# A one-core encoder layer: modulation columns of the first chunk moved ahead, later chunks of h made whole from PSUM, and high weights used first

## The chip, the cores and the metric

The kernel runs on one core of a Trainium2 chip, as one launch. The metric is the device time of that launch in microseconds (us). Three runs of the kernel before took 1886.06 to 1887.91 us, with a median of 1886.77 us. The engines are named as in the profile: PE does matrix multiplications and transposes, PEld is its loading of the stationary operand, DVE, ACT and POOL do elementwise work, and SP issues most of the transfers.

## The reference, cut to what matters

The layer mixes a convolution branch and a stick-breaking attention branch. What the change touches is its beginning, up to the projections of q, k and v:

```
mod = silu(c) @ w_ada + b_ada          # 3 x 1024 values, one row
shift, scale, gate = split(mod, 3)
h = rms_norm(x, norm_g) * (1 + scale) + shift      # x is 2048 x 1024, f32
u = h @ w_in                           # 1024 x 5632; 1536 of the columns are q, k, v
q, k = head_rms_norm(q), head_rms_norm(k)
```

All tensors are float32. The kernel keeps that precision by splitting each operand into a high part in PE's rounded format (`fp32r`) and a low part, the remainder, and by adding three products: high with high, high with low, low with high.

## The kernel before, in words

The 2048 positions are worked in four chunks of 512, the last first (ORDER is 3, 2, 1, 0). For each chunk, and for each of the eight blocks kc of 128 channels, h is kept on chip as two tiles of 128 x 512, `hhi` and `hlo`. The weights of q, k and v come in six groups of 256 columns (q0, q1, k0, k1, v0, v1), each in two pieces of four blocks, and each piece as a high and a low tile. `nat_tile` (L211) computes, for half a chunk, two results of 128 positions x 256 columns out of 24 matmuls each.

**The modulation.** Each of the 16 values needed per channel block (`mod` columns 8 + kc for the scale and kc for the shift) is a dot product of a row of `w_ada` with silu(c). `mod_col` does one column on DVE: a multiply of a 128 x 1024 tile `wa` with `ca` whose sum is accumulated. The `wa` tiles come by `wa_load` into a ring of four (NWA).

**The first chunk (the loop over kc in the middle of `trunk_kernel`).** In each turn the two columns of block kc are done on DVE, then ACT makes `b_s` and `a_s` from them, then `hf` (the modulated block, from PSUM), then `hhi`; DVE then makes `hlo`, and PE multiplies the block with q0 and q1 (24 matmuls of 128 x 256). DVE and ACT are written with `dve` and `act`, which keep the program's order on those engines, so that the next block's columns stand behind this block's `hlo`. The weights of q0 and q1 are cast (ACT) and their low parts taken (DVE) between.

**The later chunks.** `h_half` makes half a chunk (two tiles of 128 positions): the squares of x on ACT, a reciprocal square root of ten small steps on DVE (`rsqrt`), a scaling of each x tile, PE's transposes into PSUM (`x_block`, a ring of three banks, `pt`), and then `modulate` for each block of 128 x 256: `hf` on ACT from PSUM (L386), `hhi` as a cast of `hf` on DVE (L393), `hlo` on POOL (L394; on DVE for some blocks). Two halves make a chunk. Chunk 2 is made while k0 and k1 are computed for chunk 3, chunk 1 during v0 and v1, chunk 0 during the first q matmuls of chunks 2 and 1. POOL also takes the low parts of the k and v weights (L103).

What sets the order is a scheduler that takes the program's order as priority; in the built program the order on each engine is fixed. A transfer takes one of eight completion counters in turn, and waits for the transfer that had the counter before it.

After that the kernel has three long stages that the change leaves alone: the projections and the convolution (to about 800 us), attention with the remaining projections beside it, and the output projections.

## Time and profile before

| | |
|---|---|
| median of three runs | 1886.77 us |
| profiled execution | 1884.81 us |
| its span on the core | 1883.1 us |
| PE busy in the span | 1800.1 us (96%) |
| DVE, ACT, POOL busy | 1240.0, 818.6, 682.1 us |

The span is the time from the first to the last instruction in the trace; the profiled execution is 1.7 us longer, which lies around the span. A busy PE is a modelled number: matmuls overlap, and a matmul's row lasts longer than the distance to the next one. Where the rows of matmuls stand one behind the other, the distance of their starts is what one of them costs. The granted clock of PE is shown as a share of 2.4 GHz, so that 1.00 is the upper and about 0.5 the lower of its two levels.

### The profile page before, as it was taken

How to read it: one execution, taken by the hardware profiler on the slowest of the kernel's cores; microseconds unless marked ns; L12 is line 12 of the kernel's file. 1: busy time of each engine (PE TensorE's matmuls, PEld its weight loads, DVE VectorE, ACT ScalarE, POOL GpSimd, SP SyncE). 2: the span in 40 equal slices, each digit the busy share in tenths (PEclk: the TensorE clock that was granted, in tenths of full speed). 3: DMA queues.
4: the chain of work that ended last, by engine and by line, in shares of the span. 5: the costliest groups of instructions: out<-in, count | busy, mean ns of one | idle time of the engine just before them, and what ended most of it. 6: DMA issues, size and time to landing. Idle time of an engine off the chain costs nothing.

```text
span 1883.1 us, 27362 instructions
## 1 busy us (share of the span) xinstructions
PE 1800.1 (96%) x9612; PEld 1519.3 (81%) x9612; DVE 1240.0 (66%) x1757; ACT 818.6 (43%) x1904; POOL 682.1 (36%) x919
## 2 busy tenths in 40 slices
PE   5889999999999998999999999999999899999999
PEld 4788889899898887878877778787788777888887
DVE  6785577997879554467777777777777895334341
ACT  4466113223131122257776776777777753010100
POOL 0253111102112143466666666656666641010100
PEclk9999999999999999999999999999999999999999
DMA  7463511406032443342222323131322346353532
GB/s 270 139 188 106 166 40 37 132 34 173 31 104 93 157 156 118 124 148 76 90 86 78 90 76 96 62 99 65 98 76 88 120 149 218 107 162 95 162 95 79
DMA packets 117599, 211.10 MB, mean 112 GB/s; under 512 B 15442, under 2 KB 27730, under 8 KB 117460
## 3 DMA queue, kind: packets, MB, share of 16 engines
q1 hardware_dynamic: 116308, 207.24, 34.8%
q10 hardware_dynamic: 1152, 2.10, 0.3%
q8 instruction: 76, 1.25, 0.3%
q14 instruction: 63, 0.52, 0.1%
HBM read 137.98 MB, written 71.30 MB: 111 GB/s over the span
## 4 chain that ended last, share of the span: by engine, by line
PE 72%; DVE 9%; issue 6%; POOL 5%; DMA 4%; ACT 4%; SPq 1%; DVEq 0%; ACTq 0%; POOLq 0%
PE pd L115 39%; PE po L115 9%; PE p L115 8%; PE av L115 5%; PE pT L120 5%; PE z L115 5%; POOL w L933 3%; DVE sc L926 2%; POOL wlo L103 1%; ACT z L922 1%; PE pt L120 1%; DVE wa L131 1%; DVE tlo L960 1%; DMA gt<-ga 1%; DMA wl<-in_w_qkv_dram 1%
## 5 line engine op out<-in xcount | busy, mean ns | idle before, releaser
L933 POOL TENSOR_TENSOR w<-w,sc 128x512 f32<-128x512 f32 (+1 forms) x320 | 361.7, 1131 | 252.0 <-DVE sc L926 179.1
L115 PE MATMUL pd<-hhi,whi 128*128 128x512 f32 x1024 | 412.4, 403 | 1.0 <-ACT vsg L839 1.0
L115 PE MATMUL pd<-hhi,wlo 128*128 128x512 f32 x1024 | 402.0, 393 | 0.0
L115 PE MATMUL pd<-hlo,whi 128*128 128x512 f32 x1024 | 401.8, 392 | 0.0
L926 DVE TENSOR_TENSOR_SCAN sc<-z,sc,w 128x512 f32<-128x512 f32 x192 | 245.0, 1280 | 91.3 <-ACT z L922 83.7
L103 POOL TENSOR_TENSOR wlo<-wl,whi 128x512 fp32r<-128x512 f32 x88 | 129.1, 1477 | 404.8 <-ACT whi L102 404.5
L921 ACT ACTIVATE w<-z 128x512 f32<-128x512 f32 (+1 forms) x320 | 172.2, 538 | 126.9 <-PE z L115 101.3
L115 PEld LDWEIGHTS pd<-hhi,wlo 128*128 128x128 f32 x1024 | 193.0, 188 | 42.2 <-POOL wlo L103 0.2
L115 PEld LDWEIGHTS pd<-hhi,whi 128*128 128x128 f32 x1024 | 195.0, 190 | 35.2 <-ACT vsg L839 1.4
L115 PEld LDWEIGHTS pd<-hlo,whi 128*128 128x128 f32 x1024 | 193.7, 189 | 34.1
L960 DVE TENSOR_TENSOR tlo<-pT,thi 128x512 fp32r<-128x512 f32 (+1 forms) x320 | 184.0, 598 | 35.1 <-ACT thi L959 32.4
L115 PE MATMUL z<-kt,q 128*128 128x512 f32 (+2 forms) x640 | 193.1, 383 | 5.4 <-DVE sc L926 3.5
L959 ACT CAST thi<-pT 128x512 fp32r<-128x512 f32 (+1 forms) x320 | 165.3, 527 | 61.3 <-PE pT L120 58.1
L120 PE MATMUL pT<-ident,w 128*128 128x128 f32 x1088 | 172.8, 274 | 9.8 <-POOL w L933 9.4
L115 PE MATMUL pd<-whi,hhi 128*128 128x256 f32 x608 | 175.6, 289 | 5.3 <-ACT hhi L131 3.6
L120 PEld LDWEIGHTS pT<-ident,w 128*128 128x128 f32 x1088 | 137.4, 141 | 45.7 <-POOL w L933 14.5
L115 PE MATMUL pd<-wlo,hhi 128*128 128x256 f32 x608 | 174.1, 287 | 0.0
L115 PE MATMUL pd<-whi,hlo 128*128 128x256 f32 x608 | 172.8, 286 | 0.0
L922 ACT ACTIVATE z<-z 128x512 f32<-128x512 f32 (+1 forms) x320 | 171.7, 537 | 0.0
L930 DVE TENSOR_TENSOR_SCAN sc<-z,tri 128x512 f32<-128x512 f32 (+3 forms) x128 | 104.4, 819 | 53.3 <-ACT z L922 41.8
L115 PE MATMUL av<-tlo,vt 128*128 128x512 f32 (+1 forms) x320 | 123.2, 385 | 13.8 <-DVE tlo L960 10.7
L115 PEld LDWEIGHTS z<-kt,q 128*128 128x128 f32 x640 | 109.7, 189 | 25.0 <-DVE sc L926 5.1
(290 smaller groups left out, 3156.1 us busy)
## 6 DMA issues: line engine op xcount, KB each, us to landing
wl<-in_w_in_dram SPq DMA_DIRECT2D x64, 256.0 KB, 2.8
wa<-in_w_ada_dram SPq DMA_DIRECT2D x24, 512.0 KB, 4.8
wl<-in_w_qkv_dram SPq DMA_DIRECT2D x36, 256.0 KB, 2.7
xt<-in_x_n_dram SPq DMA_DIRECT2D x16, 512.0 KB, 5.0
vst<-st SPq DMA_DIRECT2D x64, 128.0 KB, 1.9
kt<-kst SPq DMA_DIRECT2D x32, 256.0 KB, 2.7
vt<-vst SPq DMA_DIRECT2D x32, 256.0 KB, 2.7
q<-qst SPq DMA_DIRECT2D x32, 256.0 KB, 2.8
```

The lines of the kernel that those rows point to most:

```text
L103: (lo_eng or nc.gpsimd).tensor_tensor(out=lo[:, s], in0=wl, in1=f(hi[:, s]), op=ALU.subtract)
L115: i = nc.tensor.matmul(*a, **k)
L120: i = nc.tensor.transpose(*a)
L131: return lambda *a, **k: tc.keep_in_program_order(getattr(self.eng, name)(*a, **k))
L921: nc.scalar.activation(out=w[:, lo:], in_=z[:, lo:], func=AF.Sigmoid, scale=HD ** -0.5)
L922: nc.scalar.activation(out=z[:, lo:], in_=z[:, lo:], func=AF.Sigmoid, scale=-HD ** -0.5)
L926: nc.vector.tensor_tensor_scan(out=s[:, 1:], data0=z, data1=w, initial=s[:, 0:1], op0=ALU.mult, op1=ALU.bypass)
L930: nc.vector.tensor_tensor_scan(out=s[:, lo + 1:], data0=z[:, lo:], data1=tri[:, :CH - lo], initial=1.0, op0=ALU.mult, op1=ALU.max)
L933: nc.gpsimd.tensor_tensor(out=w[:, lo:], in0=w[:, lo:], in1=s[:, lo:CH], op=ALU.mult)
L959: nc.scalar.copy(out=thi[:, :n], in_=pT[:, :n])
L960: nc.vector.tensor_tensor(out=tlo[:, :n], in0=pT[:, :n], in1=f(thi[:, :n]), op=ALU.subtract)
```

## The change

The first chunk's columns are done one block ahead: the four first `wa` tiles are loaded at once, `column(i)` does column i of a list of sixteen and loads the tile four columns later, and inside turn kc the two columns of block kc + 1 stand between ACT's `hhi` and DVE's `hlo` of block kc. The later chunks are made by `h_chunk`, whole: four x tiles, one reciprocal square root, and blocks of 128 x 512 of which ACT makes `hhi` and DVE makes `hf`, both from PSUM. It is a generator, so that its eight blocks can be issued in parts. In the first of the four results of each `nat_tile` pair the two products with the high weights come first for four blocks, then the product with the low weights.

```
-            mm(ps[:, i, :], rh[kc][:, t], wh, start=start, stop=False)
-            mm(ps[:, i, :], rh[kc][:, t], wl, start=False, stop=False)
-            mm(ps[:, i, :], rl[kc][:, t], wh, start=False, stop=stop)
+            for k in part:
+                mm(ps[:, i, :], (rh, rl, rh)[k][kc][:, t], (wh, wh, wl)[k],
+                   start=start and k == part[0], stop=stop and k == part[-1])
...
             for i in range(2):
-                for kc in range(KC):
-                    nat_mm(ps, w2, b, half, i, kc, kc == 0, kc == KC - 1)
+                parts = ((0, 1), (2,)) if half == i == 0 else ((0, 2, 1),)
+                for k0 in (0, 4):
+                    for part in parts:
+                        for kc in range(k0, k0 + 4):
+                            nat_mm(ps, w2, b, half, i, kc,
+                                   kc == 0 and part is parts[0],
+                                   kc == KC - 1 and part is parts[-1], part)
...
-        def h_half(g, o, pool, bufs, on_dve, xs=None):
+        def h_chunk(g, pool, on_dve, xs=None, parts=4):
             order = tc.keep_in_program_order if xs else lambda i: i
-            xs = xs or x_load(4 * g + o, 2, pool, bufs)
-            ss = pool.tile([P, 2], F32, tag="ss2", name="ss")
-            for i in range(2):
+            xs = xs or x_load(4 * g, 4, pool, NXT)
+            ss = pool.tile([P, 4], F32, tag="ss4", name="ss")
+            for i in range(4):
                 x_square(xs[i], ss[:, i:i + 1], pool, order)
             x_scaled(xs, ss, pool, order)
             for kc in range(KC):
-                hf = pool.tile([P, CH], F32, tag="hf", name="hf", bufs=6)[:, :2 * P]
-                modulate(x_block(xs, kc), hf, g, o * P, kc, (1, 0),
-                         nc.vector if kc in on_dve else nc.gpsimd)
+                hi, lo = (h[kc] for h in hT(g))
+                col = slice(kc, kc + 1)
+                ps = x_block(xs, kc)
+                hf = pool.tile([P, CH], F32, tag="hf", name="hf", bufs=6)
+                nc.scalar.activation(out=hi, in_=ps, func=AF.Identity, scale=a_s[:, col],
+                                     bias=b_s[:, col])
+                nc.vector.tensor_scalar(out=hf, in0=ps, scalar1=a_s[:, col],
+                                        scalar2=b_s[:, col], op0=ALU.mult, op1=ALU.add)
+                (nc.vector if kc in on_dve else nc.gpsimd).tensor_tensor(
+                    out=lo, in0=hf, in1=f(hi), op=ALU.subtract)
+                if kc % (KC // parts) == KC // parts - 1:
+                    yield
...
-            wa = [wa_load(j) for j in (8, 0)]
+            wa = [wa_load(j) for j in (8, 0, 9, 1)]
...
+            def column(i):
+                if i < 2 * KC:
+                    mod_col(i // 2 + (8 if i % 2 == 0 else 0), ca, wa.pop(0), dve)
+                    i += 4
+                    if i < 2 * KC:
+                        wa.append(wa_load(i // 2 + (8 if i % 2 == 0 else 0)))
+            column(0)
+            column(1)
             for kc in range(KC):
-                wa += [wa_load(j) for j in (9 + kc, 1 + kc) if kc + 1 < KC]
-                for j in (8 + kc, kc):
-                    mod_col(j, ca, wa.pop(0), dve)
...
+                column(2 * kc + 2)
+                if kc:
+                    column(2 * kc + 3)
                 dve.tensor_tensor(out=lo, in0=hf, in1=f(hi), op=ALU.subtract)
                 if kc == 0:
                     rest(wq[1], w2_q1[0])
+                    column(3)
...
-            h_half(ORDER[1], 0, hx, NXT, (), xs)
             k0 = first(w2_k0)
+            xs += x_load(4 * ORDER[1] + 2, 2, hx, NXT)
+            h = h_chunk(ORDER[1], hx, (), xs)
...
-            for o in (0, 2):
-                h_half(ORDER[3], o, hz, 4, (6, 7))
+            for _ in h_chunk(ORDER[3], hz, (6, 7)):
+                pass
```

In the built program three places move. The first is SP's queue at the start; `wa` are the modulation rows, `ba` and `ng` the bias and the norm's gain that the first block also needs. Before:

```order
L353 DMA xt<-in_x_n_dram 128x1024 x4
L424 DMA wa<-in_w_ada_dram 128x1024 x2
L191 DMA ba<-in_b_ada_dram 128x24
L191 DMA ng<-in_norm_g_dram 128x8
L424 DMA wa<-in_w_ada_dram 128x1024 x2
```

And of the change:

```order
L359 DMA xt<-in_x_n_dram 128x1024 x4
L424 DMA wa<-in_w_ada_dram 128x1024 x4
L191 DMA ba<-in_b_ada_dram 128x24
L191 DMA ng<-in_norm_g_dram 128x8
L191 DMA gain<-in_q_gain_dram 128x1
```

Two loads of 512 KB have moved ahead of the two small ones.

The second is DVE's queue in the first chunk: `ba_441` or `ba_445` is a small step that reads `ng`, the rows with `wa,mod` are columns, `wlo` and `whx` are low parts of the weights of q0 and q1, `hlo` is the low part of a block. Before:

```order
L131 SCALAR_TENSOR_TENSOR ba_441<-ba,ng 128x8
L131 SCALAR_TENSOR_TENSOR wa,mod<-wa,ca 128x1024 x2
L131 TENSOR_TENSOR wlo<-wl,whi 128x512 x2
L131 TENSOR_TENSOR hlo_3_309<-hf,hhi_3_301 128x512
L131 TENSOR_TENSOR whx<-hf,whx 128x512 x2
L131 SCALAR_TENSOR_TENSOR wa,mod<-wa,ca 128x1024 x2
L131 TENSOR_TENSOR hlo_3_310<-hf,hhi_3_302 128x512
L131 TENSOR_TENSOR wlo<-wl,whi 128x512 x2
L131 SCALAR_TENSOR_TENSOR wa,mod<-wa,ca 128x1024 x2
L131 TENSOR_TENSOR hlo_3_311<-hf,hhi_3_303 128x512
```

And of the change:

```order
L131 SCALAR_TENSOR_TENSOR ba_445<-ba,ng 128x8
L131 SCALAR_TENSOR_TENSOR wa,mod<-wa,ca 128x1024 x2
L131 TENSOR_TENSOR wlo<-wl,whi 128x512 x2
L131 SCALAR_TENSOR_TENSOR wa,mod<-wa,ca 128x1024
L131 TENSOR_TENSOR hlo_3_309<-hf,hhi_3_301 128x512
L131 TENSOR_TENSOR whx<-hf,whx 128x512 x2
L131 SCALAR_TENSOR_TENSOR wa,mod<-wa,ca 128x1024 x3
L131 TENSOR_TENSOR hlo_3_310<-hf,hhi_3_302 128x512
L131 TENSOR_TENSOR wlo<-wl,whi 128x512 x2
L131 SCALAR_TENSOR_TENSOR wa,mod<-wa,ca 128x1024 x2
L131 TENSOR_TENSOR hlo_3_311<-hf,hhi_3_303 128x512
```

Each block's two columns now stand before the low part of the block ahead of it.

The third is POOL's queue while chunk 2 is made: `whx` are the low parts of the v weights, `hlo_2` those of chunk 2. Before, the second half of the chunk and what follows it:

```order
L103 TENSOR_TENSOR whx<-wl,whx 128x512 x2
L394 TENSOR_TENSOR hlo_2_325<-hf,hhi_2_317 128x256
L394 TENSOR_TENSOR hlo_2_326<-hf,hhi_2_318 128x256
L394 TENSOR_TENSOR hlo_2_327<-hf,hhi_2_319 128x256
L394 TENSOR_TENSOR hlo_2_328<-hf,hhi_2_320 128x256
L394 TENSOR_TENSOR hlo_2_329<-hf,hhi_2_321 128x256
L394 TENSOR_TENSOR hlo_2_330<-hf,hhi_2_322 128x256
L394 TENSOR_TENSOR hlo_2_331<-hf,hhi_2_323 128x256
L394 TENSOR_TENSOR hlo_2_332<-hf,hhi_2_324 128x256
L103 TENSOR_TENSOR whx<-wl,whx 128x512 x3
```

And of the change, the whole chunk:

```order
L103 TENSOR_TENSOR whx<-wl,whx 128x512 x12
L403 TENSOR_TENSOR hlo_2_325<-hf,hhi_2_317 128x512
L403 TENSOR_TENSOR hlo_2_326<-hf,hhi_2_318 128x512
L103 TENSOR_TENSOR whx<-wl,whx 128x512
L403 TENSOR_TENSOR hlo_2_327<-hf,hhi_2_319 128x512
L403 TENSOR_TENSOR hlo_2_328<-hf,hhi_2_320 128x512
L103 TENSOR_TENSOR whx<-wl,whx 128x512
L403 TENSOR_TENSOR hlo_2_329<-hf,hhi_2_321 128x512
L403 TENSOR_TENSOR hlo_2_330<-hf,hhi_2_322 128x512
L403 TENSOR_TENSOR hlo_2_331<-hf,hhi_2_323 128x512
L103 TENSOR_TENSOR whx<-wl,whx 128x512
```

The four last low weights (v1's) now stand between and behind the chunk's eight low parts, where chunk 2's halves were done before them.

## Rows read from the trace of the kernel before

**Rows 1.** Busy time by stage: stretch, length, each engine's busy us, PEclk, DMA share, GB/s

```profile
19.30:64.10 44.80, 33.42 (x221) 30.67 (x220) 26.81 (x46) 19.25 (x39) 2.52 (x2) 0.89 0.54 176
64.10:87.40 23.30, 20.35 (x162) 19.55 (x162) 19.69 (x49) 10.50 (x19) 10.23 (x8) 0.99 0.59 181
87.40:166.10 78.70, 67.17 (x532) 64.38 (x533) 59.48 (x159) 54.60 (x139) 37.27 (x45) 0.98 0.52 161
166.10:400.00 233.90, 233.90 (x1270) 203.21 (x1270) 168.81 (x210) 56.74 (x219) 41.56 (x30) 1.00 0.29 88
```

**Rows 2.** Chain of waits in order of time, at the beginning's end: start, length, what

```profile
171.85 0.44 PE pt L120 x4
```

**Rows 3.** DVE in the first chunk, by time: start, length, instruction, idle before it

```profile
14.77 0.17 DVE L131 SCALAR_TENSOR_TENSOR ba<-ba,ng 128x8 f32<-128x8 f32 x1 [0.46 <-DMA ng<-in_norm_g_dram]
...
17.14 1.29 DVE L131 TENSOR_TENSOR wlo<-wl,whi 128x512 fp32r<-128x512 f32 x2
...
32.51 1.22 DVE L131 SCALAR_TENSOR_TENSOR wa<-wa,ca 128x1024 f32<-128x1024 f32 x1
...
33.65 1.22 DVE L131 SCALAR_TENSOR_TENSOR wa<-wa,ca 128x1024 f32<-128x1024 f32 x1
...
36.98 0.69 DVE L131 TENSOR_TENSOR hlo<-hf,hhi 128x512 fp32r<-128x512 f32 x1 [2.10 <-ACT hhi L131]
...
59.73 0.69 DVE L131 TENSOR_TENSOR hlo<-hf,hhi 128x512 fp32r<-128x512 f32 x1 [2.10 <-ACT hhi L131]
```

**Rows 4.** ACT in one turn of the first chunk, by time

```profile
34.91 0.29 ACT L131 ACTIVATE b_s<-mod,ba 128x1 f32<-128x1 f32 x1 [3.05 <-DVE wa L131]
...
36.33 0.62 ACT L131 CAST hhi<-hf 128x512 fp32r<-128x512 f32 x1
```

**Rows 5.** SP's issues at the start, by time

```profile
9.26 0.33 SPq L191 DMA_DIRECT2D ng<-in_norm_g_dram  x1
11.70 0.80 SPq L424 DMA_DIRECT2D wa<-in_w_ada_dram  x2
```

**Rows 6.** Landing times of the wa loads, from the view of that tile

```profile
DMA to landing us min/median/max: 3.3/4.9/8.2
```

**Rows 7.** Busy time in short stretches of the first chunk, columns as in rows 1

```profile
12.00:16.00 4.00, 2.21 (x10) 1.98 (x11) 3.37 (x11) 3.11 (x4) 0.00 (x0) 1.00 1.05 379
...
20.00:24.00 4.00, 4.00 (x21) 3.82 (x20) 3.51 (x7) 0.79 (x3) 0.00 (x0) 0.57 0.76 257
...
32.00:40.00 8.00, 6.71 (x52) 6.22 (x52) 5.90 (x11) 3.04 (x6) 0.00 (x0) 1.00 0.82 274
```

**Rows 8.** PE in a turn of the first chunk, by time: start, length, instruction

```profile
32.14 0.28 PE L115 MATMUL pd<-wlo,hhi 128*128 128x256 f32 x1
32.26 0.28 PE L115 MATMUL pd<-whi,hhi 128*128 128x256 f32 x1
```

**Rows 9.** Groups by form up to 170 us: count | busy us, mean ns | idle before

```profile
L393 DVE CAST hhi<-hf 128x256 fp32r<-128x256 f32 x48 | 22.7, 506 | 2.7 <-ACT hf L386 2.7
...
L89 DVE SCALAR_TENSOR_TENSOR nx2t<-nx2y 128x2 f32<-128x2 f32 x18 | 6.6, 366 | 0.4
...
L394 POOL TENSOR_TENSOR hlo<-hf,hhi 128x256 fp32r<-128x256 f32 x40 | 30.5, 780 | 35.6 <-DVE hhi L393 12.6 <-issue 12.0 <-DVE nx2y L92 6.7
L103 POOL TENSOR_TENSOR whx<-wl,whx 128x512 fp32r<-128x512 f32 x16 | 20.4, 1285 | 79.1 <-ACT whx L102 77.0 <-DVE ssq L338 2.1
```

**Rows 10.** The cast of hhi alone: count, shortest, median and longest in ns

```profile
L393 DVE CAST hhi<-hf x48: 277/288/999, 91.5 to 167.1; 128x256 fp32r<-128x256 f32 x48
```

**Rows 11.** POOL, and DVE beside it, by time

```profile
92.60 5.91 POOL L394 TENSOR_TENSOR hlo<-hf,hhi 128x256 fp32r<-128x256 f32 x8 [0.23 <-DVE hhi L393]
97.13 0.68 DVE L312 TENSOR_TENSOR qlo<-pt,qhi 128x512 fp32r<-128x512 f32 x1
```

**Rows 12.** ACT on a tile of x of a later chunk: square, read of its sum, scaling

```profile
82.30 1.05 ACT L358 ACTIVATE sq<-xt 128x1024 bf16<-128x1024 f32 x1
83.26 0.19 ACT L358 ACTIVATION_READ_ACCUMULATOR sq<-xt 128x1 f32 x1
...
89.36 1.15 ACT L367 ACTIVATE xt<-xt,nx2y 128x1024 f32<-128x1024 f32 x1 [4.01 <-DVE nx2y L92]
```

More of the change, by code (lines that the diff above doesn't have):

```diff
@@ L198, in piece, with nat_mm @@
             return load_piece(wpb if npiece[0] % 3 == 0 else wpa, src)
-        def nat_mm(ps, w2, b, half, i, kc, start, stop):
+        def nat_mm(ps, w2, b, half, i, kc, start, stop, part=(0, 2, 1)):
             rh, rl = hT(b)
@@ L378, in x_block @@
             return ps[:, :n]
-        def modulate(src, hf, g, o, kc, act, lo_eng):
-            t = slice(o, o + src.shape[1])
-            hi, lo = (h[kc][:, t] for h in hT(g))
-            a_, b_ = a_s[:, kc:kc + 1], b_s[:, kc:kc + 1]
-            if act[0]:
-                nc.scalar.activation(out=hf, in_=src, func=AF.Identity, scale=a_, bias=b_)
-            else:
-                nc.vector.tensor_scalar(out=hf, in0=src, scalar1=a_, scalar2=b_,
-                                        op0=ALU.mult, op1=ALU.add)
-            if act[1]:
-                nc.scalar.copy(out=hi, in_=hf)
-            else:
-                nc.vector.tensor_copy(hi, hf)
-            lo_eng.tensor_tensor(out=lo, in0=hf, in1=f(hi), op=ALU.subtract)
-        def h_half(g, o, pool, bufs, on_dve, xs=None):
+        def h_chunk(g, pool, on_dve, xs=None, parts=4):
             order = tc.keep_in_program_order if xs else lambda i: i
-            xs = xs or x_load(4 * g + o, 2, pool, bufs)
-            ss = pool.tile([P, 2], F32, tag="ss2", name="ss")
-            for i in range(2):
+            xs = xs or x_load(4 * g, 4, pool, NXT)
+            ss = pool.tile([P, 4], F32, tag="ss4", name="ss")
+            for i in range(4):
                 x_square(xs[i], ss[:, i:i + 1], pool, order)
@@ L536, in trunk_kernel @@
             norm_at_once(qk_ps[0], 0, g0, hx)
-            h_half(ORDER[1], 0, hx, NXT, (), xs)
             k0 = first(w2_k0)
+            xs += x_load(4 * ORDER[1] + 2, 2, hx, NXT)
+            h = h_chunk(ORDER[1], hx, (), xs)
             norm_at_once(qk_ps[1], 1, g0, hx)
+            next(h)
+            next(h)
             w2_v0 = [hx_piece(w_qkv[4, i], "w1") for i in range(2)]
             k1 = first(w2_k1)
-            h_half(ORDER[1], 2, hx, NXT, ())
+            next(h)
+            next(h)
             norm_at_once(k0, 2, g0, hx)
@@ L545, in trunk_kernel @@
             w2_v1 = [hx_piece(w_qkv[5, i], "wa") for i in range(2)]
-            h_half(ORDER[2], 0, hx, NXT, (0, 4))
+            h = h_chunk(ORDER[2], hx, (0, 4))
+            next(h)
+            next(h)
             norm_at_once(k1, 3, g0, hx)
             first_v(first(w2_v1), 5)
-            h_half(ORDER[2], 2, hx, NXT, (0, 4))
+            next(h)
+            next(h)
         h0 = hst.enter_context(tc.tile_pool(name="h0", reuse_waits="tile", bufs=1))
```

## The prediction

> **What bounds the kernel now.** I read the stages first, then the chain of waits in order of time, then each engine's rows by time where PE is idle. From 166.1 us on PE is busy for all of the 233.9 us up to 400 us, at the upper clock [rows 1]. The change works ahead of that only, so the question is at what time PE comes to that point. I call it M: the start of the 48 matmuls that precede the transposes of q at 171.85 us [rows 2]. They belong to the last chunk's q, and their starts lie 0.12 us apart [rows 8], so M = 171.85 - 48 x 0.12 = 166.1 us. All that comes before M earlier moves the end by as much, if nothing else takes over.
>
> Two stretches lie before M. In the first chunk (19.3 to 64.1 us) a turn of the loop takes about 5 us. After its two columns end, DVE waits 2.10 us in a turn [rows 3], for the chain on ACT from b_s at 34.91 to the end of hhi at 36.95 [rows 4]; the next columns stand behind the low part that waits. PE does the 24 matmuls of a turn in 24 x 0.12 = 2.9 us [rows 8], plus 0.44 us for four transposes [rows 2], and idles for the rest: it is busy for 33.42 of the 44.8 us [rows 1]. From 64.1 to M (102.0 us) PE has 384 matmuls for k and v of chunk 3, 192 for q of two more chunks, 96 transposes of x and 32 of q and k. At 0.12 and 0.11 us each that is 69.1 + 14.1 = 83.2 us. The other 18.8 us are waits, most of them for h.
>
> **The change, part by part.**
>
> *The start.* The small load ng is what DVE waits for at 14.77 [rows 3]; it was issued at 9.26 and landed 5.4 us later [rows 5]. Now two loads of 512 KB stand ahead of it. ng takes the counter of the first wa, and is issued when the third and fourth wa were in the kernel before, about 12.2 us [rows 5]. At the 379 GB/s of that stretch [rows 7] the 1.05 MB ahead of it take 2.8 us. If they hold it back by that alone it lands at 14.7 + 2.8 = 17.5. If it needs the 5.4 us that it needed before, from its later issue, it lands at 17.6; were it held by neither, it would land as before, and the cost would be nothing. I take 17.6, a delay of 2.9 us; the range is 0 to 5.7, the upper end if it takes as long as the slowest wa, 8.2 us [rows 6]. *The Trainium skill ("DMA: Bandwidth & Descriptors", on queues, rings and completion order) says that descriptors are taken in ring order on each of the DMA engines. By that rule the delay is the 2.8 us; a queue that let the small load pass would give nothing. That rule speaks against this edit.*
>
> *The loop.* A column costs 1.14 us (32.51 to 33.65), a low part of a block or of half a weight tile 0.69 us by its row and 0.61 from start to start, since two at 17.14 take 1.29 with their overlap [rows 3]. With the columns in front, DVE has work in the whole of ACT's 2.1 us: two columns take 2.3 us. From ng to the last column DVE's queue holds 16 columns (18.3 us), eight low parts of weights (4.9 us) and seven of blocks (4.3 us), together 27.5 us. After the last column ACT's 2.1 us stand bare once, so that the eighth low part starts 27.5 - 0.6 + 2.1 = 29.0 us after ng's step. Before it was 59.73 - 14.77 = 45.0 us [rows 3]. That is 16.0 us less, and 13.1 us with the late start: 46.6 us instead of 59.7. PE is now nearly as slow: block 0 can be multiplied from about 22 us, block 1 from 27.7 (its second column stands behind the weights), and 27.7 + 7 x 3.3 = 50.8 us. A cast of a k weight stands on ACT ahead of the last block (0.6 us, in part hidden). I take 51.3 us for the end of the first chunk's matmuls instead of 64.1: 12.8 us earlier. Bounds: 7 us if the loads of wa hold the loop (below), 15.5 us if ng isn't late. The granted clock was 0.57, near the lower of its two levels (1.2 and 2.4 GHz), in 20 to 24 us, after PE had been busy for 2.21 of the 4 us up to 16 [rows 7]. Such a stretch costs about 4 x 0.43 = 1.7 us; I count none as gained or added.
>
> *h by whole chunks.* On DVE 48 casts of 506 ns (24.3 us) go and 24 steps of 128 x 512 from PSUM come. No such step is in the trace. The nearest row is the subtraction from PSUM of the same shape, 0.68 us [rows 11]: 16.3 us. The lower end is the cast's 288 ns for half as many values [rows 10], so 0.45 us (10.8 us in all); the upper end is below, with the rivals. Six chains of ten small steps become three; of their costliest kind 9 of 18 go, which is 3.3 us [rows 9], and less of the others. ACT has 24 steps instead of 48, of about the 0.62 us of a cast of this shape [rows 4]; POOL 20 low parts of 1.285 us instead of 40 of 0.780 [rows 9], 25.7 for 31.2 us. So every engine has less, but h comes later within a chunk: four tiles of x must be squared before the first is scaled. Followed from T, the end of the first chunk's matmuls:
> - k0 keeps its 2.9 us of waits (23.3 less 20.35 [rows 1]), for the weights and the first normalised q; the high weights first save up to 1 us of them, and the q chain then waits as much longer. With 192 matmuls and 16 transposes k1 ends at T + 27.7.
> - Chunk 2: on ACT the square of the fourth x tile stands behind the squares of k1's last result, about 0.6 us, and its own 1.25 us [rows 12]: T + 29.5. Ten small steps of 0.366 [rows 9] and two scalings on ACT of 1.15 [rows 12] follow: T + 35.5, and 35.8 with the transposes. PE has 32 matmuls of v0 and 12 transposes (5.2 us) until then, so it waits 3.0 us.
> - POOL now has eight low parts of h and four of weights in one row, 12 x 1.285 = 15.4 us [rows 9], from about T + 37.8 when the first block is there, and the last weights come last, at T + 53.2. PE reaches them after 86 matmuls, 28 transposes (13.4 us) and about a microsecond of waits for blocks, at T + 50.2, and waits 3.0 us.
> - Chunks 1 and 0 have the same chain from the last square on, 1.25 + 3.7 + 2.3 = 7.2 us, with 5.8 and 4.8 us of matmuls beside it: 1.5 and 2.5 us.
>
> That is 12.9 us of waits instead of 18.8, so M is T + 83.2 + 12.9 = T + 96.1, against T + 102.0: 5.9 us earlier. Bounds: each wait can be half as long or half as long again (6.5 us each way), so from -1 to 12 us.
>
> *High weights first* moves matmuls in a result and adds none. It hides 1.3 us of POOL at k0's start and k1's, which is in the waits above; later PE has no wait for a weight, so it is worth nothing there.
>
> **The sum.** M comes 12.8 + 5.9 = 18.7 us earlier. The profiled execution is 1884.81 us (span 1883.1 and 1.7 around it), so 1866.1. The median is 1.96 us above that execution: 1868.1 us.
>
> **Who holds DVE.** The cast took 288 ns in its median and 999 at most [rows 10], and its mean of 506 is paid where POOL works at the same time. The subtraction from PSUM took 0.68 us at 97.13, in the middle of POOL's row from 92.60 to 98.51 [rows 11]. Whether hf behaves as the one or the other decides the third rival. *The Trainium skill ("SBUF — State Buffer", on who interferes with whom) says that DVE and POOL share a pair of ports, which one of them holds for a whole instruction, and that an operation of DVE with one SBUF operand outside the two-port modes doesn't need it. By that rule hf isn't held and the third rival is void; without it, it would be likelier than I make it. The row at 97.13 agrees, for another operation.*
>
> **Rivals.**
> - *The loads hold the loop.* 12 wa, four halves of weights and one for k are 7.6 MB, to be moved from about 19 us. At the 274 GB/s of 32 to 40 us [rows 7] they take 27.7 us, and the last columns could be done at 48.7 + 2; T would be about 56, the gain 8 + 6 = 14 us: 1873. For it: two in flight gave 4.9 us in the median [rows 6], and the ring gives back a tile only after its column. Against: four are in flight now, and 379 GB/s has been seen [rows 7].
> - *The second stretch gives nothing*, because the whole chunks' later start costs what the shorter queues save: 12.8 us, 1874. For it: POOL's row ahead of v1 and the fourth square.
> - *Slower: POOL holds each new step of DVE.* If it does, each of 24 waits for one of POOL's 1.285 us: 31 us more on DVE. That is in series with PE's next transposes, since three banks of PSUM hold the blocks. PE has matmuls for about 10 us of it. The second stretch then loses 21 us and gains 5.9 elsewhere, and with the first it ends at 1884.81 + 1.96 - 12.8 + 15 = 1889. It decides if more than 0.75 us per block is bare. Against it: the row at 97.13.
> - *The gain is given back later*: the convolution on DVE, 168.8 of 233.9 us busy after M [rows 1], could be the bound behind PE. Then 1886. Against: it starts with PE's first results after M and moves with them.
>
> **How the numbers follow.** About 0.2% (3.8 us) is what a measurement can tell from no change. My forecast with its own range (1861 to 1871.5) has 0.55, the held loop 0.15, nothing from the second stretch 0.15, slower through POOL 0.06, given back 0.05; 0.04 is for a larger gain than 26 us. Faster are the first three and the last, less a small share that ends near the bound: 0.88. Same takes most of the given back, and a little of the others: 0.06. Slower 0.06. The range reaches from both ends of the first stretch (12.8 to 15.5) and the second (5.9 to 12) together, 1859, to a held loop (8) with the worst of the second (-1), 1879.8.
>
> **What would show it.** ng's step on DVE near 17.6 us; the low parts of blocks about 3 us apart without the wait of 2.1 us; the first chunk's matmuls ended near 51 us; hf of about 0.68 us, whatever POOL does; waits of PE of 3 us before chunk 2's transposes and in v1's first result; the transposes of q now at 171.85 near 153. A wa column that waits for its load, hf steps of over 1 us, or PE idle after M would make it wrong.

## The result, and the profile after

The changed kernel takes 1872.26 us in the median of four runs (1868.88 to 1877.81); before is 1886.74 us beside it. The ratio is 0.9925 (95% interval 0.9901 to 0.9950). The forecast was 1868.1 us (1859.0 to 1879.8). In a second set (e3 below) the same kernel took 1875.88 us, ratio 0.9944 (0.9931 to 0.9957): it is faster by 10.7 to 14.5 us, and the forecast was 18.7. The profiled execution is the slowest of the first four: 1877.81 us, span 1876.1.

The stages after, cut at the same points of the program as [rows 1]: the first chunk's matmuls end at 54.1 us (64.1 before), and M is at 155.5 us (166.1 before). Columns: the stretch and its length; busy time and count of PE, PEld, DVE, ACT, POOL; granted clock, DMA share, GB/s.

```profile
19.30:54.10 34.80, 29.06 (x212) 27.38 (x213) 29.43 (x48) 21.09 (x42) 3.67 (x2) 1.00 0.71 243
54.10:155.50 101.40, 89.39 (x715) 86.30 (x714) 62.24 (x150) 60.19 (x144) 42.33 (x34) 0.98 0.53 167
155.50:400.00 244.50, 243.93 (x1352) 213.07 (x1351) 180.06 (x226) 59.20 (x244) 43.75 (x30) 1.00 0.28 85
```

So of the 10.6 us at M the first stretch gave 10.0 (12.8 forecast) and the second 0.6 (5.9 forecast). The second stretch doesn't hold quite the same work in the two: in the kernel before, PE did the first twelve matmuls of k0 in the idle time of the first chunk, from 42.08 us on, and had 660 matmuls between the first chunk's end and the second transposes of the last chunk's q; the changed kernel has 672 there. The twelve cost 1.4 us at 0.12 us each. The first of them, in the kernel before:

```profile
42.08 0.38 PE L115 MATMUL pd<-whx,hhi 128*128 128x256 f32 x1 [1.93 <-ACT whx L102]
```

PE is again busy behind M, but for 0.6 us.

DVE in the first chunk, the rows that answer to [rows 3] (start, duration, line, operation, operands, and the idle time ahead with what ended it):

```profile
17.52 0.17 DVE L131 SCALAR_TENSOR_TENSOR ba<-ba,ng 128x8 f32<-128x8 f32 x1 [3.33 <-DMA ng<-in_norm_g_dram]
...
34.48 0.68 DVE L131 TENSOR_TENSOR hlo<-hf,hhi 128x512 fp32r<-128x512 f32 x1
35.57 0.69 DVE L131 TENSOR_TENSOR whx<-wl,whx 128x512 fp32r<-128x512 f32 x1 [0.41 <-ACT whx L131]
37.03 0.69 DVE L131 TENSOR_TENSOR whx<-wl,whx 128x512 fp32r<-128x512 f32 x1 [0.78 <-ACT whx L131]
...
39.36 1.23 DVE L131 SCALAR_TENSOR_TENSOR wa<-wa,ca 128x1024 f32<-128x1024 f32 x1 [0.49 <-DMA wa<-in_w_ada_dram]
...
40.51 0.69 DVE L131 TENSOR_TENSOR hlo<-hf,hhi 128x512 fp32r<-128x512 f32 x1
...
43.68 1.50 DVE L131 TENSOR_TENSOR hlo<-hf,hhi 128x512 fp32r<-128x512 f32 x1 [0.20 <-ACT hhi L131]
...
46.25 1.21 DVE L131 SCALAR_TENSOR_TENSOR wa<-wa,ca 128x1024 f32<-128x1024 f32 x1
...
47.39 1.76 DVE L131 TENSOR_TENSOR hlo<-hf,hhi 128x512 fp32r<-128x512 f32 x1
49.57 0.69 DVE L131 TENSOR_TENSOR hlo<-hf,hhi 128x512 fp32r<-128x512 f32 x1 [0.42 <-ACT hhi L131]
```

ACT and POOL in the same time; ACT's casts there are of the second halves of q's weights, POOL's steps are the low parts of k0's first weights:

```profile
34.91 0.62 ACT L131 CAST whx<-wl 128x512 fp32r<-128x512 f32 x1 [1.18 <-DMA wl<-in_w_qkv_dram]
36.38 0.62 ACT L131 CAST whx<-wl 128x512 fp32r<-128x512 f32 x1 [0.85 <-DMA wl<-in_w_qkv_dram]
```

```profile
43.21 1.42 POOL L103 TENSOR_TENSOR whx<-wl,whx 128x512 fp32r<-128x512 f32 x1 [41.81 <-ACT whx L102]
46.35 2.25 POOL L103 TENSOR_TENSOR whx<-wl,whx 128x512 fp32r<-128x512 f32 x1 [1.72 <-DVE wa L131]
```

ACT's 2.10 us per turn is gone but for 0.20 and 0.42. In its place DVE waits 1.7 us for weights and for one wa, and two low parts take 1.50 and 1.76 us for 0.69 where POOL's 43.21 and 46.35 run beside them.

What PE waited for from the first chunk's end to the transposes of q, in the kernel before and after (total, times, longest):

```profile
PE pt L120 <- DVE xt L369: 7.0, 4, 2.8
PE pd L115 <- POOL whx L103: 3.2, 5, 1.1
PE pt L120 <- ACT sq L358: 1.6, 1, 1.6
PE pt L120 <- DVE qn L292: 1.2, 1, 1.2
PE pt L120 <- DVE qlo L308: 0.6, 1, 0.6
PE pd L115 <- ACT whx L102: 0.5, 1, 0.5
PE pt L120 <- ACT hf L386: 0.3, 1, 0.3
```

```profile
PE pt L120 <- DVE xt L375: 5.0, 3, 2.1
PE pd L115 <- POOL whx L103: 3.8, 5, 2.0
PE pt L120 <- DVE qn L298: 1.8, 1, 1.8
PE pd L115 <- ACT whx L102: 1.3, 2, 0.9
PE pd L115 <- POOL u L651: 0.6, 1, 0.6
```

The lists add up to 14.4 us before and 12.5 after: fewer waits for tiles of x, more for weights.

### The profile page after: what moved, and what is told of

Its sections match the earlier page's. It is cut to its first block, busy times and chain, and to the rows that moved or that the text cites. A ratio compares the mean times of both kernels' runs of the same rounds, so it can differ in the third digit from the quotient of the medians.

```text
span 1876.1 us, 27226 instructions
## 1 busy us (share of the span) xinstructions
PE 1797.0 (96%) x9612; PEld 1517.0 (81%) x9612; DVE 1228.2 (65%) x1696; ACT 812.8 (43%) x1880; POOL 681.3 (36%) x899
## 4 chain that ended last, share of the span: by engine, by line
PE 72%; DVE 8%; POOL 6%; issue 5%; DMA 5%; ACT 4%; SPq 1%; DVEq 0%; ACTq 0%; POOLq 0%
PE pd L115 38%; PE po L115 9%; PE p L115 8%; PE av L115 5%; PE pT L120 5%; PE z L115 5%; POOL w L952 3%; DVE sc L945 2%; POOL wlo L103 1%; ACT z L941 1%; DMA xt<-in_x_n_dram 1%; PE pt L120 1%; DVE tlo L979 1%; DMA wa<-in_w_ada_dram 1%; DMA gt<-ga 1%
## 5 line engine op out<-in xcount | busy, mean ns | idle before, releaser
L120 PEld LDWEIGHTS pT<-ident,w 128*128 128x128 f32 x1088 | 137.5, 141 | 45.9 <-POOL w L952 14.5
L115 PE MATMUL pd<-whi,hhi 128*128 128x256 f32 x608 | 169.7, 287 | 3.6 <-ACT hhi L131 1.9
L115 PE MATMUL pd<-whi,hlo 128*128 128x256 f32 x608 | 167.0, 285 | 2.3 <-DVE hlo L131 1.7
L115 PE MATMUL pd<-wlo,hhi 128*128 128x256 f32 x608 | 154.0, 284 | 0.0
```

The lines of the kernel that those rows point to most:

```text
L115: i = nc.tensor.matmul(*a, **k)
L120: i = nc.tensor.transpose(*a)
```

## The experiments

Each was measured against before in the same set of runs; e1 to e4, e5 to e8 and e9 to e12 are a set each. "End" is the end of the first chunk's matmuls; "q" the start of the second four transposes of the last chunk's q (the instruction at 177.88 us before). Between them lie 132 transposes in all, and 672 matmuls but for before and e2 with 660 and e8 with 669. "Rest" is from q to the span's end: the same work in all, though with the weights in each kernel's own order, since `nat_tile` makes later results too. All three are from one profiled execution each, which need not be a typical one (e2's is the slowest of its ten runs, e5's the fastest of its six); the medians and intervals are of all runs.

| run | end | q | end to q | rest | median, before | ratio (95%) |
|---|---|---|---|---|---|---|
| before | 64.1 | 177.88 | 113.8 | 1705.2 | | |
| changed | 54.1 | 167.28 | 113.2 | 1708.8 | 1872.26, 1886.74 | 0.9925 (0.9901 to 0.9950) |
| e3 changed again | 54.3 | 164.72 | 110.4 | 1708.7 | 1875.88, 1886.55 | 0.9944 (0.9931 to 0.9957) |
| e1 loop | 54.0 | 166.73 | 112.7 | 1707.0 | 1873.47, 1886.55 | 0.9935 (0.9923 to 0.9947) |
| e2 whole chunks | 62.6 | 181.34 | 118.7 | 1711.3 | 1891.55, 1886.55 | 1.0019 (1.0008 to 1.0031) |
| e5 loop, chunks | 53.4 | 168.76 | 115.4 | 1703.1 | 1880.66, 1888.94 | 0.9948 (0.9934 to 0.9962) |
| e6 loop, halves from PSUM | 53.8 | 165.19 | 111.4 | 1706.4 | 1873.74, 1888.94 | 0.9920 (0.9907 to 0.9933) |
| e7 loop, chunks the old way | 52.8 | 169.91 | 117.1 | 1707.8 | 1877.44, 1888.94 | 0.9938 (0.9925 to 0.9951) |
| e4 changed, ng early | 50.9 | 162.64 | 111.7 | 1709.4 | 1872.93, 1886.55 | 0.9921 (0.9909 to 0.9933) |
| e8 loop, ng early, late casts | 51.1 | 164.20 | 113.1 | 1708.7 | 1873.74, 1888.94 | 0.9920 (0.9907 to 0.9933) |
| e9 as e4, two q tiles | 51.0 | 165.26 | 114.3 | 1705.7 | 1872.77, 1887.60 | 0.9925 (0.9911 to 0.9939) |
| e10 changed, low parts on DVE | 53.4 | 162.45 | 109.0 | 1707.3 | 1870.26, 1887.60 | 0.9910 (0.9897 to 0.9924) |
| e11 | 51.4 | 162.35 | 111.0 | 1709.1 | 1869.42, 1887.60 | 0.9911 (0.9895 to 0.9926) |
| e12 | 50.5 | 163.27 | 112.8 | 1706.0 | 1869.48, 1887.60 | 0.9908 (0.9895 to 0.9922) |

The changed kernel's own two executions differ by 2.8 us from end to q, so a smaller difference in that column proves nothing by itself.

**e1: the loop alone** (the hunks of wa, column() and its calls; nothing else of the change)

```diff
-            wa = [wa_load(j) for j in (8, 0)]
+            wa = [wa_load(j) for j in (8, 0, 9, 1)]
...
+                column(2 * kc + 2)
+                if kc:
+                    column(2 * kc + 3)
```

> Only the loop of the first chunk is changed (columns one block ahead, four loads of wa ahead of ng); h by halves and the order of the weights are as before. Theory 1, from the trace of the changed kernel: there the first matmul of k0 came at 54.1 us instead of 64.6, and nearly all of its 10.6 us at the transposes of q (161.09 for 171.69) are this edit. Then here too k0 starts near 54, the transposes of q come near 161 to 162, and the time is about 1876.5. Theory 2, the split of the prediction: the loop gives two thirds and the second stretch the rest, so that without the second edit a third of the gain is missing: transposes of q at 165 to 166, time near 1880. Theory 3: the halves of h cover the shorter loop better than whole chunks do; the transposes come before 160 and the time is below 1873.

The first chunk ends as in the changed kernel, and the time is 13.1 us under before. Theory 1 holds: the loop alone gives what the whole change gives (10.7 and 14.5 us in its two sets). The list of PE's waits in the second stretch is as short as the changed kernel's 12.5 us, too, with h still made by halves and the weights in the old order:

```profile
PE pt L120 <- DVE xt L369: 7.9, 4, 2.2
PE pd L115 <- POOL whx L103: 2.1, 4, 1.1
PE pt L120 <- DVE qn L292: 1.4, 1, 1.4
PE pt L120 <- DVE qrt L89: 1.0, 1, 1.0
```

**e2: whole chunks alone** (the hunks of h_chunk and its calls)

```diff
-            h_half(ORDER[1], 0, hx, NXT, (), xs)
+            h = h_chunk(ORDER[1], hx, (), xs)
```

> Only h of the later chunks is changed (whole chunks, high part and f32 value both from PSUM); the loop of the first chunk and the order of the weights are as before. Theory 1: from the end of the first chunk to the transposes of q the changed kernel took 107.0 us for 107.6, so this edit is worth about 0.6 us: transposes of q near 171, time 1886, within 0.2% of before. Theory 2, the prediction: 5.9 us, transposes near 166, time near 1881. Theory 3: it costs by itself (weights of v that come 3 us late behind the stores of q), hidden so far by the earlier loop: transposes after 173, time above 1888. The step for hf takes 0.75 to 0.83 us in each of them.

5.0 us slower than before, interval above 1: theory 3 in its time. From end to q it takes 118.7 us for 113.8. The waits listed for PE add up to no more than before (13.5 us for 14.4; POOL's low weights are 4.7 of them, for 3.2), but PE is busy longer with the same work: 104.60 us for 99.30, at a granted clock of 0.94 for 0.98. Before, then e2:

```profile
64.10:177.88 113.78, 99.30 (x793) 0.98 0.50 153
```

```profile
62.60:181.34 118.74, 104.60 (x794) 0.94 0.48 147
```

So the reason that theory 3 gave, late weights of v, isn't what fills the 4.9 us of this execution. Nor is the lower clock what makes e2 slow as a rule: over the whole span its ten runs were granted 0.990 in the mean, as were the sixteen of before, and they are 5.0 us slower in the median all the same.

**e3: the changed kernel again**

> The changed kernel once more, unchanged. Its four runs lay 9 us apart (1868.9 to 1877.8) where those of the kernel before lay 1.9 apart, and the profiled one was the slowest. Theory 1: the transposes of q come at 161.1 within 0.5 us in this execution too, and the spread arises later: from there to the end it took 3.2 us longer than in the kernel before, lost between 700 and 800 us and around 1500 us, where the clock falls to its lower level; another execution has these stretches in other places. Theory 2: the spread arises ahead of the transposes (loads of wa and weights that land at other times), which then come at 155 to 158 in a faster execution.

The difference of the two executions arises ahead of q, as theory 2 has it: q comes 2.6 us earlier in this one (164.72 for 167.28), and from q on the two take the same time (1708.7 and 1708.8). Against the profiled execution of before both lose about 3.5 us behind q.

**e4: ng and ba behind the first pair of wa**

```diff
-            wa = [wa_load(j) for j in (8, 0, 9, 1)]
+            wa = [wa_load(j) for j in (8, 0)]
             ba = load_const(b_ada, 24, "ba")
             ng = load_const(norm_g, KC, "ng")
+            wa += [wa_load(j) for j in (9, 1)]
```

> The changed kernel with ba and ng loaded behind the first pair of wa, as before the change, and the third and fourth wa behind them. Theory 1: the step of DVE that waits for ng goes from 17.5 back to about 14.8, DVE's queue is the bound of the loop, and all comes 2.7 us earlier: k0 at 51.4, transposes of q at 158.4, time 2.7 us below the changed kernel. Theory 2: the loop waits for its loads anyway (the weights' second halves, the wa of the third and fourth column, now issued later): k0 stays within 1 us of 54.1 and the time within 1 us of the changed kernel's.

The step of DVE is back:

```profile
14.61 0.17 DVE L131 SCALAR_TENSOR_TENSOR ba<-ba,ng 128x8 f32<-128x8 f32 x1 [0.60 <-DMA ng<-in_norm_g_dram]
```

The first chunk ends 3.2 us earlier than in the changed kernel, as theory 1 has it; the median is 3.0 us under e3, of the same set, and the intervals just overlap.

**e5: loop and whole chunks, old order of the weights** (e1 and e2 together)

```diff
             for i in range(2):
-                parts = ((0, 1), (2,)) if half == i == 0 else ((0, 2, 1),)
...
+                for kc in range(KC):
+                    nat_mm(ps, w2, b, half, i, kc, kc == 0, kc == KC - 1)
```

> The loop of the first chunk and h by whole chunks are changed, the order of the weights in a result is as before. So far the loop alone gave 1873.5 us, whole chunks alone 1891.6 (5 us slower than before), and all three edits 1875.9. Theory 1: whole chunks cost here too, about 2.4 us on top of the loop, and the high weights first are worth nothing: 1875.9, transposes of q at 158.5 to 161. Theory 2: the high weights first make up for a part of what whole chunks cost: without them 1878 or more, and PE waits for POOL's low weights at the start of k0 and v0 by 1 us or more longer. Theory 3: with the earlier loop whole chunks cost nothing and the difference was the spread of the runs: 1873.5.

115.4 us from end to q, and only 8.3 us under before. This points to theory 2, though its interval overlaps both of the changed kernel's. PE waits for POOL's low weights eight times (5.4 us for 3.8), and steps along POOL's low parts of the last chunk:

```profile
150.77 0.39 PE L115 MATMUL pd<-whi,hhi 128*128 128x256 f32 x1 [0.44 <-ACT hhi L393]
153.02 0.39 PE L115 MATMUL pd<-whi,hlo 128*128 128x256 f32 x1 [0.75 <-POOL hlo L397]
154.26 0.39 PE L115 MATMUL pd<-whi,hlo 128*128 128x256 f32 x1 [0.18 <-POOL hlo L397]
155.50 0.38 PE L115 MATMUL pd<-whi,hlo 128*128 128x256 f32 x1 [0.17 <-POOL hlo L397]
```

Its POOL row begins at 151.70, when PE is already there; in the changed kernel POOL's row begins at 148.93 and PE comes to this result at 154.4. So the new order of the weights shortens PE's wait for POOL where chunks are whole (5.4 and 1.5 us for POOL's two kinds of low parts here, 3.8 and none in the changed kernel). What it is worth in time, 115.4 against 113.2 and 110.4, isn't clear of the spread.

**e6: the loop, and halves with both values from PSUM**

```diff
-            if act[0]:
-                nc.scalar.activation(out=hf, in_=src, func=AF.Identity, scale=a_, bias=b_)
...
-                nc.vector.tensor_copy(hi, hf)
+            nc.scalar.activation(out=hi, in_=src, func=AF.Identity, scale=a_, bias=b_)
+            nc.vector.tensor_scalar(out=hf, in0=src, scalar1=a_, scalar2=b_,
+                                    op0=ALU.mult, op1=ALU.add)
```

> The loop is changed; h of the later chunks is made by halves as before, but its high part (ACT) and its f32 value (DVE) both come from PSUM, 48 steps of 128 x 256 each; order of the weights as before. Compared with the loop alone (1873.5). Theory 1: what whole chunks cost is the size of the step (four tiles of x squared before the first block, longer rows of POOL), so this one doesn't have it: 1873.5 within 1.5, the 48 steps of DVE shorter than 0.6 us each and not longer where POOL works. Theory 2: what costs is DVE's read of PSUM while ACT reads the same bank: 1876 or more, DVE's steps of 0.6 us and more. Theory 3: it gains, since ACT's f32 value and DVE's cast that POOL holds up (506 ns in the mean for 288) leave the chain: 1871 or less.

15.2 us under before in its set, e1 13.1 in another: between theories 1 and 3. Clear is that it is not theory 2. The steps of DVE, busy time and mean:

```profile
L386 DVE TENSOR_SCALAR hf<-pt,a_s,b_s 128x256 f32<-128x256 f32 x48 | 24.0, 537 | 6.2 <-ACT hhi L385 6.0
```

**e7: the loop, and whole chunks the old way** (e5 with ACT's f32 value and DVE's cast)

```diff
-                nc.scalar.activation(out=hi, in_=ps, func=AF.Identity, scale=a_s[:, col],
+                nc.scalar.activation(out=hf, in_=ps, func=AF.Identity, scale=a_s[:, col],
                                      bias=b_s[:, col])
-                nc.vector.tensor_scalar(out=hf, in0=ps, scalar1=a_s[:, col],
-                                        scalar2=b_s[:, col], op0=ALU.mult, op1=ALU.add)
+                nc.vector.tensor_copy(hi, hf)
```

> The loop is changed; h of the later chunks is made by whole chunks, but as before the change ACT writes the f32 value and DVE casts it to the high part from SBUF, 24 steps of 128 x 512 each; order of the weights as before. Compared with the loop and whole chunks from PSUM (e5) and the loop alone (1873.5). Theory 1 (the size of the step costs): as e5 or a little slower, 1876 to 1878. Theory 2 (reading PSUM costs): 1873.5 or less. In both the casts show what POOL does to DVE: those beside a step of POOL take up to a step of POOL longer (1.29 us), the others about 0.5 us.

117.1 us from end to q, 4.4 more than e1: this points to theory 1, that the size of the step costs, but doesn't show it. The listed waits are 12.6 us for e1's 12.4; PE is busy longer with the same work, 104.35 us for 100.38, at a granted clock of 0.96 for 0.98. By the medians the interval overlaps that of e1 as well as that of e5. The casts took from 0.41 us to 1.52 beside POOL, 961 ns in the mean:

```profile
L395 DVE CAST hhi<-hf 128x512 fp32r<-128x512 f32 x24 | 22.0, 961 | 6.8 <-ACT hf L393 6.8
```

**e8: the loop, ng early, the second halves of q's weights one block later**

```diff
-                if kc in (1, 3):
-                    cast(wq, (w2_q0, w2_q1)[kc // 2][1])
-                    rest(wq, (w2_q0, w2_q1)[kc // 2][1])
+                if kc in (2, 4):
+                    cast(wq, (w2_q0, w2_q1)[kc // 2 - 1][1])
+                    rest(wq, (w2_q0, w2_q1)[kc // 2 - 1][1])
```

> The loop alone (h by halves, weights in the old order), with ba and ng loaded behind the first pair of wa, and the casts and low parts of the second halves of q's weights one block later (behind blocks 2 and 4 instead of 1 and 3). Theory 1: DVE's queue is the bound of the loop, ng costs 2.7 to 3.2 us and the wait for the weights' second half 2.0 us (low part of block 4 came 6.0 us behind that of block 3, for 3.2 us elsewhere): k0 at 49 instead of 54.0, time 5 us under the loop alone, 1868.5. Theory 2: behind them PE is the bound, with 24 matmuls and four transposes a turn, and the two low parts that POOL holds for 1 us each: k0 at 50 to 51, time 1870 to 1871.

The first chunk ends at 51.1 us, where e4 without the later casts has 50.9: they give nothing. ACT's casts of k0's weights now stand ahead of a block's high part, and DVE waits 1.67 us for that. The end and the time are nearer to theory 2, but in this row DVE still waits for ACT, and PE for DVE.

**e9: as e4, every second pair of q and k in another place**

```diff
+            if pool and pr:
+                hi, lo = (lambda t: (t[:, :CH], t[:, CH:]))(
+                    pool.tile([P, D], F32R, tag="ca", name="q2", bufs=1))
```

> The changed kernel with ng early (e4: transposes of q at 156.5, 13.6 us under before) and the high and low parts of every second pair of transposed q or k in another place of SBUF (that of the columns' vector, free by then), so that they don't wait for the stores of the pair before. Theory 1: in the changed kernel ACT waits 0.8, 3.2 and 2.8 us for the stores of q, the squares of chunk 2's tiles stand behind that, SP's queue with the weights of v0 too; then PE's waits between 78 and 88 us (5 us with the step itself) shrink to about 2, transposes near 153.5, time about 3 us below e4. Theory 2: the loads of x and weights are late by themselves (DMA share 0.83 in that stretch), and the stores only stand among them: less than 1 us.

Theory 1 fell short: q comes 2.6 us later than in e4, not 3 earlier, and the time is e4's (ratio 0.9925 and 0.9921), as theory 2 has it. PE waits 5.4 us for POOL's low weights instead of 3.8, and 3.2 us for hf, which e4 doesn't show; for tiles of x it waits 1.8 us instead of 3.0. So other waits took the place of those that went.

**e10: half of the low parts on DVE**

```diff
-            h = h_chunk(ORDER[1], hx, (), xs)
+            h = h_chunk(ORDER[1], hx, (1, 3, 5, 7), xs)
...
-            h = h_chunk(ORDER[2], hx, (0, 4))
+            h = h_chunk(ORDER[2], hx, (0, 2, 4, 6))
...
-            for _ in h_chunk(ORDER[3], hz, (6, 7)):
+            for _ in h_chunk(ORDER[3], hz, (1, 3, 5, 7)):
```

> The changed kernel with half of the low parts of h of the three later chunks on DVE (four of eight in each) instead of none, two and two; all else as changed. Theory 1: POOL's row of twelve steps of 1.29 us between 92 and 108.6 us makes PE wait 2.2 us for v1's low weights and 0.9 us at 156; with four steps less it ends 5 us earlier, both waits go, the transposes come 2 to 3 us earlier (158.5 from 161.1, or 156 from 158.5). Theory 2: DVE, which then does 24 steps of 0.8 us and 12 low parts of up to 1.3 us beside POOL, holds the blocks back by as much: same time within 1 us, and PE waits for DVE's low parts or for the next bank.

Theory 1: the shortest stretch of all (109.0 us), 17.3 us under before, and an interval below that of the changed kernel's second set. The wait for v1's low weights is gone from PE's list, and the one behind u too:

```profile
PE pt L120 <- DVE xt L375: 4.3, 3, 1.9
PE pt L120 <- DVE qn L298: 1.8, 1, 1.8
PE pd L115 <- ACT whx L102: 1.7, 2, 0.9
PE pd L115 <- POOL whx L103: 1.4, 3, 0.6
```

**e11: the loop, ng early, halves from PSUM, high weights first; e12: the same with e9's second place** (of e11's edit the part that moves ng is shown, against the changed kernel; the halves are e6's hunk)

```diff
-            wa = [wa_load(j) for j in (8, 0, 9, 1)]
+            wa = [wa_load(j) for j in (8, 0)]
...
+            wa += [wa_load(j) for j in (9, 1)]
```

> The loop, ng early, halves of h with both values from PSUM, and high weights first. Halves from PSUM on top of the loop gave 15.2 us under before (transposes of q at 159.0), and ng early brought the end of the first chunk's matmuls from 54.1 to 50.9. Theory 1 (the terms add up): transposes near 155.8, 18.4 us under before, some 1868 where before is 1886.6: faster than the changed kernel by about 4 us. Theory 2: half of what ng brings is waited away for loads of x and weights, which come no earlier: 16.8 us under before.

> As e11, with the second place for every other pair of q and k. Theory 1: by halves PE had no wait for v's weights at 78 to 88 us, only for tiles of x (2.3 us at 77) and 3.7 us at 90 for a block behind the normalising of q and k; stores aren't what holds them, so it is worth less than 1 us: as e11. Theory 2: the stores hold SP's queue and ACT in the same way, and the waits at 77 and 90 shrink by 2 to 3 us: 20 to 21 us under before.

18.2 and 18.1 us under before, nearest to theory 1 in both; e11's two theories are 1.6 us apart, less than its interval can tell. Both are below the changed kernel in its second set (0.9911 and 0.9908, intervals up to 0.9926 and 0.9922, against 0.9931 and more); with its first set the intervals overlap. Low parts on DVE and ng early together were not tried.

## Why the number came out near, and the split did not

- **The start.** Right: 17.52 us for 17.6 forecast, 2.75 us later than before [rows 3], and e4 takes it back to 14.61. ng was issued at 11.97 us (about 12.2 forecast) instead of 9.26 [rows 5] and landed 5.45 us later, where it had taken 5.4. In the chain of waits (start, time to landing, what):

```profile
11.97 5.45 DMA ng<-in_norm_g_dram
```

  So the later issue, the second of the prediction's readings, gives the whole delay. The Trainium skill ("DMA: Bandwidth & Descriptors", on queues, rings and completion order) says that each DMA engine takes descriptors in ring order, and by that rule the delay was to be 2.8 us. The number agrees, but the trace can't tell this rule from the later issue, and e4 takes back both at once.
- **The loop.** The mechanism was right: the columns hide ACT's 2.1 us, and e1 shows that this edit carries the change. The size was off: the eighth low part starts at 49.57 us, not 46.6, and the first chunk ends at 54.1, not 51.3. The term that failed is "27.5 us of DVE's queue", which has every step at its undisturbed duration and no load late. The last column ends at 47.4 us, where the sum has 17.5 + 27.5 - 0.6 = 44.4. Of the 3.0 us between, the rows above give 1.7 of waits for loads, 0.2 for ACT and 0.8 for the sixth low part beside POOL. ACT's chain behind the last column then takes the 2.1 us that I forecast, and the 1.1 us that the seventh low part loses to POOL lie within it. But PE waits for that low part, and its last 40 matmuls (4.8 us) stand behind its end at 49.15:

```profile
49.21 0.39 PE L115 MATMUL pd<-whi,hlo 128*128 128x256 f32 x1 [0.84 <-DVE hlo L131]
```

- **hf.** 806 ns in the mean for 0.68 forecast, and POOL does not hold it: five in 4.17 us within POOL's row.

```profile
150.40 4.17 DVE L401 TENSOR_SCALAR hf<-pt,a_s,b_s 128x512 f32<-128x512 f32 x5 [0.17 <-ACT hhi L399]
```

```profile
148.93 7.97 POOL L403 TENSOR_TENSOR hlo<-hf,hhi 128x512 fp32r<-128x512 f32 x6 [15.93 <-DVE hf L401]
```

  The third rival is void. The two low parts of 1.50 and 1.76 us in the loop are the other side of it: they read both operands from SBUF, and POOL's steps beside them took 1.42 and 2.25 us for 1.285. Each in turn waits there: POOL's step of 46.35 begins 0.1 us after a column, which also reads two operands from SBUF, and ends at 48.60, 1.2 us after the column; the low part of 47.39 ends 0.55 us after that. The Trainium skill ("SBUF — State Buffer", on who interferes with whom) says that a DVE instruction with two SBUF inputs contends with a GpSimd instruction that reads SBUF, one with a single input outside the two-port modes doesn't. The trace agrees with both halves; I had used the second only.
- **The second stretch.** This is the step that failed: "12.9 us of waits instead of 18.8". The 12.9 came out (12.5), though the sum leaves out the microsecond of waits for blocks that the list itself names. The 18.8 was wrong: it was the stretch less its matmuls, with all 384 matmuls for k and v counted into it. Twelve of them stood in the first chunk's idle time before, so 81.8 us of work and 20.2 us of other time made up the 102.0. PE's own list of waits has 14.4 of the 20.2; the other 5.8 us (the clock's lower level, changes between transposes and matmuls) are not waits, and stay (5.7 after). So the waits fell by 1.9 us, and the twelve matmuls took 1.4 of that back. The 1.9 isn't due to whole chunks either, since e1 has 12.4 us of waits without them. Within the 12.5 the places differ: the tiles of chunk 2 cost 1.6 us for 3.0, v1's low weights 1.95 for 3.0, chunk 1 2.1 for 1.5, chunk 0 1.3 for 2.5, and 2.6 us between 82 and 93 us for v0's weights weren't foreseen. The rival "the second stretch gives nothing" is what happened, with 0.15.
- **Whole chunks and high weights first.** I gave the first the 5.9 us and the second nothing. For the second my reason was that later PE has no wait for a weight, against the 3.0 us for v1's weights in my own list. The runs show that whole chunks cost, in the old order of weights: by the medians e2 is 5.0 us over before, its interval above 1, and e5 6.9 us over e6, which has the same data flow by halves, the intervals just clear of each other. In the profiles they lengthen the stretch by 4.9 us (e2 to before), 4.0 (e5 to e6) and 4.4 (e7 to e1). With the new order chunks take 113.2, 110.4, 111.7 and 114.3 us instead of 115.4 (e5): it seems to give back from 1.1 to 5.0 us, which one profile of e5 and overlapping intervals don't prove. Both values from PSUM give 1.3 (e6 to e1) and 1.7 us (e5 to e7), no more than two executions of one kernel differ. What makes chunks dear is open in part. POOL's row is one cause: e10 takes 1.4 to 4.2 us off by shortening it, and PE's waits for POOL's low weights fall from 3.8 to 1.4 us. In the profiles of e2 and e7 the listed waits are hardly longer than with halves, and a lower clock lengthens the stretch (0.94 for 0.98, 0.96 for 0.98); but e5 is slower than e6 at a higher one (0.99, e6 0.97), and the medians of e2 and before differ at the same one.
- **After M.** I counted nothing there. In the profile the changed kernel needs 1720.6 us from M to the end, before 1717.0. 1.6 us of that lie here, between about the same places of the program (before, then after):

```profile
645.00:760.00 115.00, 107.20 (x570) 0.96 0.38 131
```

```profile
634.40:751.00 116.60, 107.15 (x556) 0.94 0.38 128
```

  PE is busy for the same time, with longer waits and a lower clock. Nothing marks this as a cost of the change: the rest, with the same work in all the kernels, took from 1703.1 (e5, which has the loop and whole chunks) to 1711.3 us, and the profiled execution of before had the second shortest. But with one profile of before this isn't shown, and the order of the weights is not the same there. Why the rest varies stays open; nothing was run on it.

So the number was near because the loop is 10 us of it and the range was wide; the second term was a difference against a wrong base. Both medians of the changed kernel, 1872.26 and 1875.88, lie outside the range of my own forecast (1861 to 1871.5, with 0.55) and beside the 1874 of the rival with 0.15: that the whole range held them is to the credit of its width, not of the sum.

## What to carry to other kernels

Take the waits of a stretch from the list of waits of the engine that bounds it, on both sides of a forecast; the stretch less its work holds more than waits, and the difference of the two is then the gain that doesn't come. Count too which work stands in the stretch: idle time that a change removes may have held some of the next stage's. A step made larger, as the whole chunks here, has fewer of its fixed costs but a later first result, and longer rows on the engine behind it: measure the size and the new data flow apart, in more than one profile each. In a loop whose bound engine has no gap left, a neighbour that slows its steps (POOL here, 0.8 and 1.1 us) and a load that lands late (1.7 us) are terms of the sum.

## What the runs showed of the hardware

- The same kernel in two executions had a stretch at the lower clock in different places. In the first, PE was granted 0.57 in 114 to 118 us, in e3 1.00 in the same microseconds and 0.57 in 87 to 91 us. First the changed kernel, then e3:

```profile
114.00:118.00 4.00, 3.83 (x20) 0.57 0.81 233
```

```profile
114.00:118.00 4.00, 3.98 (x35) 1.00 0.70 189
87.00:91.00 4.00, 3.48 (x16) 0.57 0.70 263
```

  In the one PE had just waited 1.95 us for v1's low weights and 2.12 for chunk 1's tiles, in the other for v0's weights. Both executions have the waits for v0's and v1's weights; the clock was low behind the ones in one and behind the others in the other.
- The 24 steps of DVE of 128 x 512 from PSUM to SBUF took 0.80 or 0.81 us each, in POOL's rows and outside them. Of before's 48 casts within SBUF, half that size, 28 took 0.28 to 0.30 us and 19 took 0.80 to 1.00: held or not held, and little between.
